# A SwiGLU FFN split into two stages: gate and up by Strassen's seven block products, down summed whole in PSUM

## The chip, the core and the metric

The kernel runs on one core of one Trainium2 chip. The metric is the time of one execution on the device in microseconds (us). Engines are named as in the profile: PE is TensorE's matmul, PEld its weight load, DVE is VectorE, ACT is ScalarE, POOL is GpSimd, SP is SyncE, whose queue issues nearly all DMAs.

## The reference, cut to what matters

One layer of a transformer-like trunk with 256 context tokens and 2048 latent tokens, D = 1024 features and D_FF = 2816 hidden features, all in float32. The token mixer is the same in both kernels; the change is in the last four lines.

```python
def rmsnorm(x, g):
    y = x * lax.rsqrt(jnp.mean(x * x, axis=-1, keepdims=True) + EPS)
    return y * g

def sandwich_block(x, mod, g_norm, mixer, w_gu, w_down):
    sh1, sc1, gt1, sh2, sc2, gt2 = mod
    h = rmsnorm(x, g_norm[0]) * (1.0 + sc1) + sh1
    m, extra = mixer(h)
    x = x + gt1 * rmsnorm(m, g_norm[1])
    h = rmsnorm(x, g_norm[2]) * (1.0 + sc2) + sh2
    gate, up = jnp.split(h @ w_gu, 2, axis=-1)       # (2304, 1024) @ (1024, 2 * 2816)
    f = (jax.nn.silu(gate) * up) @ w_down            # (2304, 2816) @ (2816, 1024)
    x = x + gt2 * rmsnorm(f, g_norm[3])
    return x, extra
```

## The kernel before

Every float32 operand of a large product is split into a high part (`F32R`, a copy by ACT) and a low part (the rest, a subtraction by DVE); `split` does both. A product is three matmuls for each 128 features of its contraction (`mm3`: high by high, high by low, low by high), summed in PSUM. All matmuls are recorded on one line, L37, since they go through the helper `InOrder`; the tile names tell them apart.

The program runs the input projection (`phase_b`, `phase_ac`), the three token mixers, the output projection (`phase_out`) and the FFN (`phase_ffn`) one after the other. `phase_out` writes the FFN's input, transposed (features on the partitions), to DRAM in six blocks of 384 tokens (`h2_d`), and the residual stream to `x1_d`. While it runs, `ffn_ahead` loads the first block and the first weights.

`phase_ffn` takes the 2304 tokens in three passes of 768 (`tb`), each of two blocks of 384 (`b`). The 22 chunks of 128 hidden features are taken in groups of four (the last has two). For each chunk `ffn_w` loads and splits 1024 x 128 weights of gate and as many of up (tiles `GH`, `GL`), and `product` makes, for each block, a gate tile and an up tile in PSUM (`p`, 24 matmuls each, 128 weights by 384 tokens), then `sg` = silu(gate) * up, and its two parts `ah`, `al` in SBUF. After a group, its four chunks are contracted with the rows of `w_down` (`dh`, `dl`): for each of 6 token tiles and 2 column halves twelve matmuls of 512 columns into `pd`, which DVE then adds to an accumulator in SBUF (`fa`, L1796 and L1798). After the last group `finish` norms, scales, adds the residual and stores the token tile.

The order: tiles come from pools that rotate over a fixed number of buffers, and the scheduler of the tile framework sets the order on each engine by priority and readiness, except where an `InOrder` engine is switched on (`pe.on`, `sp.on`), whose instructions keep the order of the program. Before, PE's is off in `phase_ffn`. Every engine takes its own queue strictly in order.

## Time and profile before

| | |
|---|---|
| time, median of 3 runs | 3910.35 us (3907.43 to 3915.01) |
| the profiled execution: span from first to last instruction | 3906.9 us; the page gives no separate time for it |
| TensorE clock granted, mean | 0.983 |
| PE busy | 3730.9 us, 95% |
| PEld busy | 3293.7 us, 84% |
| DVE, ACT, POOL busy | 2019.6, 1544.1, 376.4 us |
| the FFN in the span | about 2229 us to the end |

Busy time of PE is the sum of the durations of pipelined matmuls whose ends are modelled, so the distance between two starts is the better price of a matmul. In a group line, the first number after the bar is the busy time of all its instructions in us, the second the mean of one in ns. In the view by stretches, each engine's busy us is followed by its number of instructions.

### The profile page before, as it was taken

To read this page: it belongs to the slowest core of one execution; us is meant where nothing else is said; L and a number is where in the kernel's file an instruction comes from. 1 tells how busy PE (TensorE), PEld (TensorE's weight loads), DVE (VectorE), ACT (ScalarE), POOL (GpSimd) and SP (SyncE) were. 2 spreads that over 40 slices of the span, in tenths; PEclk is the share of its full clock that TensorE was granted. 3 is DMA by queue.
4 is the path that set the end of the run, shared out by engine and by line. 5 is a ranking of instruction groups with operands and counts; after the bars stand their busy time and mean duration, and the time that the engine had idled before them with its cause. 6 is when DMAs were issued, how large, how long until landed. Compare 5 with 4: busy or idle time off the path is not lost.

```text
span 3906.9 us, 64049 instructions
## 1 busy us (share of the span) xinstructions
PE 3730.9 (95%) x25318; PEld 3293.7 (84%) x25318; DVE 2019.6 (52%) x4488; ACT 1544.1 (40%) x3184; POOL 376.4 (10%) x691
## 2 busy tenths in 40 slices
PE   8997989879999999899999999999999999999998
PEld 5887889867777777688877899999999999999997
DVE  4794576689655555478755433333533323533323
ACT  4223322246666666557756522222322112322221
POOL 0002322620000000010024200000000000000000
PEclk9998999989999999999999999999999999999999
DMA  7556877741211111264336532222521122522211
GB/s 265 204 199 190 259 212 218 191 108 46 55 51 51 51 51 51 67 176 109 86 115 206 185 103 65 65 65 64 166 67 60 60 60 66 171 65 65 60 60 54
DMA packets 580862, 436.07 MB, mean 112 GB/s; under 512 B 247042, under 2 KB 519793, under 8 KB 578385
## 3 DMA queue, kind: packets, MB, share of 16 engines
q1 hardware_dynamic: 577776, 428.37, 36.7%
q8 instruction: 199, 3.26, 0.4%
q10 hardware_dynamic: 2624, 3.55, 0.3%
q14 instruction: 103, 0.84, 0.1%
q0 software_dynamic: 160, 0.05, 0.0%
HBM read 313.80 MB, written 118.05 MB: 111 GB/s over the span
## 4 chain that ended last, share of the span: by engine, by line
PE 48%; issue 31%; DVE 10%; ACT 4%; DMA 4%; POOL 3%; SPq 1%; POOLq 0%; ACTq 0%; DVEq 0%
PE p L37 9%; PE pso L37 8%; PE pt L37 7%; PE po L37 6%; PE pd L37 5%; PE rx L37 3%; DVE stmp L843 2%; PE Sa L37 2%; PE Sb L37 2%; PE S L37 2%; DVE mx L1220 2%; DVE sW L844 1%; PE m L37 1%; ACT P L1228 1%; DMA y<-oa 1%
## 5 line engine op out<-in xcount | busy, mean ns | idle before, releaser
L37 PE MATMUL p<-fhi,GH 128*128 128x384 f32 x2112 | 711.0, 337 | 5.1 <-DVE raw L1674 3.1
L37 PE MATMUL p<-flo,GH 128*128 128x384 f32 x2112 | 711.0, 337 | 0.3 <-DVE flo L1691 0.3
L37 PE MATMUL p<-fhi,GL 128*128 128x384 f32 x2112 | 710.0, 337 | 1.1 <-DVE GL L1691 1.1
L1034 ACT ACTIVATE PT<-pt 128x512 f32<-128x512 f32 (+1 forms) x600 | 332.3, 554 | 256.0 <-PE pt L37 249.2
L37 PEld LDWEIGHTS p<-fhi,GH 128*128 128x128 f32 x2112 | 397.3, 188 | 6.6 <-ACT raw L1623 3.3
L37 PEld LDWEIGHTS p<-fhi,GL 128*128 128x128 f32 x2112 | 397.3, 188 | 2.1 <-DVE GL L1691 1.8
L37 PEld LDWEIGHTS p<-flo,GH 128*128 128x128 f32 x2112 | 397.4, 188 | 1.7 <-DVE flo L1691 0.7
L1744 ACT ACTIVATE sg<-p 128x384 f32<-128x384 f32 x132 | 64.4, 488 | 681.0 <-PE p L37 681.0
L37 PE MATMUL po<-PT,V 128*64 128x256 f32 (+1 forms) x3072 | 314.8, 342 | 2.2 <-ACT PT L1034 1.9
L37 PE MATMUL pd<-dh,ah 128*128 128x512 f32 x792 | 309.3, 390 | 5.8 <-DVE fa L1798 5.5
L37 PE MATMUL pso<-whi,hi 128*128 128x384 f32 (+2 forms) x864 | 289.0, 334 | 26.2 <-ACT whi L255 13.7
L37 PE MATMUL pd<-dh,al 128*128 128x512 f32 x792 | 308.7, 390 | 0.0
L37 PE MATMUL pd<-dl,ah 128*128 128x512 f32 x792 | 308.5, 390 | 0.0
L1691 DVE TENSOR_TENSOR GL<-raw,GH 128x1024 fp32r<-128x1024 f32 x132 | 161.7, 1225 | 274.8 <-ACT GH L1690 274.6
L37 PE MATMUL pt<-ident,P 128*128 128x128 f32 x1752 | 284.9, 280 | 14.9 <-ACT PT L1034 7.9
L37 PE MATMUL pso<-whi,lo 128*128 128x384 f32 (+2 forms) x864 | 282.7, 327 | 6.4 <-DMA lo<-hl 6.3
L37 PE MATMUL pso<-wlo,hi 128*128 128x384 f32 (+2 forms) x864 | 282.7, 327 | 0.6 <-DVE wlo L256 0.5
L37 PEld LDWEIGHTS pt<-ident,P 128*128 128x128 f32 x1752 | 200.3, 141 | 94.3 <-ACT PT L1034 36.1
L1798 DVE TENSOR_TENSOR fa<-pd,fa 128x512 f32<-128x512 f32 x180 | 124.0, 690 | 264.9 <-PE pd L37 263.3
L37 PEld LDWEIGHTS po<-PT,V 128*64 128x64 f32 x3072 | 181.5, 137 | 79.3 <-issue 33.8
L1745 DVE TENSOR_TENSOR sg<-sg,p 128x384 f32<-128x384 f32 x132 | 73.0, 553 | 266.7 <-PE p L37 266.6
L1690 ACT ACTIVATE GH<-raw 128x1024 fp32r<-128x1024 f32 x132 | 139.8, 1061 | 144.8 <-PE p L37 125.6
(298 smaller groups left out, 6916.0 us busy)
## 6 DMA issues: line engine op xcount, KB each, us to landing
raw<-in_w_gu_dram SPq DMA_DIRECT2D x264, 256.0 KB, 3.6
raw<-in_w_down_dram SPq DMA_DIRECT2D x66, 512.0 KB, 3.7
wm<-in_w_mod_dram SPq DMA_DIRECT2D x48, 512.0 KB, 4.2
hi<-hh SPq DMA_DIRECT2D x36, 512.0 KB, 5.2
lo<-hl SPq DMA_DIRECT2D x36, 512.0 KB, 6.3
st<-ptk SPq DMA_DIRECT2D x18, 768.0 KB, 4.2
rst<-st SPq DMA_DIRECT2D x36, 384.0 KB, 5.3
hh<-hi SPq DMA_DIRECT2D x6, 1536.0 KB, 6.1
```

What stands on the lines that cost most here:

```text
L37: r = f(*x, **kw)
L843: v.tensor_tensor(tv, M[:n, c0:c1, c0:i], M[:n, c0:i, i].unsqueeze(1).to_broadcast([n, m, k]), ALU.mult)
L844: v.tensor_reduce(M[:n, c0:c1, i], tv, AX.X, ALU.add)
L1034: self.nc.scalar.activation(out, p, AF.Copy)
L1220: nc.vector.tensor_reduce(mx[:, i:i + 1], S[:, :hi_ - lo_], AX.X, ALU.max)
L1228: nc.scalar.activation(P[:, lo_:hi_], Ss[i][:, :hi_ - lo_], AF.Exp, bias=mx[:, 3:4], accum_out=sm[:, i:i + 1])
L1690: self.nc.scalar.activation(hi, raw, AF.Copy)
L1691: self.nc.vector.tensor_tensor(lo, raw, hi.bitcast(F32), ALU.subtract)
L1744: nc.scalar.activation(sg, ps[0], AF.Silu)
L1745: nc.vector.tensor_tensor(sg, sg, ps[1], ALU.mult)
L1798: nc.vector.tensor_tensor(facc[i][:, s], p, facc[i][:, s], ALU.add)
```

## The change

The FFN becomes two functions, `ffn_up` and `ffn_down`, with `silu(gate) * up` in DRAM between them (`a_d`, one tensor for each token tile).

`ffn_up` takes the same three passes of 768 tokens. For one chunk of 128 hidden features (one unit) the product is seen as a 2x2 block product: rows gate and up, contraction halves of 512 features, columns the two blocks of 384 tokens. Strassen's form in Winograd's variant needs seven block products of 12 matmuls (84 matmuls) in place of eight (96). Its operands are sums of blocks. Those of the weights are made for each unit: four POOL additions on 128x512 (`S`), and seven splits of 128x512 (`gop`, 10 buffers). Those of the tokens are made once for each pass by `prep_h` (`hop`, seven tiles without a second buffer, each filled in two halves `kk` of 128x768; temporaries `ht`, some of them made by POOL). The results are put together from three PSUM tiles X, Y and Z by five DVE additions of 384 columns that read PSUM (`p1`, `u2`, `u3`), two silus and a copy on ACT, and two POOL multiplications of 384 columns; six DMAs write the unit's result. PE keeps the order of the program: in it the last two products of a unit follow the first product of the next one, but not at the end of a pass.

`ffn_down` goes over the column halves `n` outermost. For each it loads and splits the 22 chunks of `w_down` once (`wd`, 24 buffers, raw tiles `wr` 4), and for every token tile `t` it loads and splits the activations in two pieces (`ar`, `ao`, 128x1408, 3 buffers) and sums 66 matmuls of 512 columns in one PSUM tile. The first half's result goes to DRAM (`f_d`); the second half's turn does the norm, the residual and the store. The program text of the other functions differs only by comments.

```diff
     def ffn_ahead(self, t):
         if 4 <= t < 12 and t % 2 == 0:
...
-        if t == 13:
-            self.first = [self.ffn_w(0, k4) for k4 in range(2)]
+        if t == 10:
+            self.sp.dma_start(self.hr1, self.h2_d[1])
+        if t == 12:
+            self.w_raw(0, self.wr0)
...
+    def ffn_up(self):
...
+            gp = es.enter_context(tc.tile_pool(name="u_g", bufs=10))
...
+            def prep_h(tb):
+                for kk in range(2):
...
+                    def put(n, x):
+                        self.split(H[n][:, 0, ks], H[n][:, 1, ks], x)
...
+                    t2 = tmp()
+                    tt(t2, B22, t1, ALU.subtract)
+                    put(6, t2)
+                    put(5, t1)
+                    t3 = tmp()
+                    gp_.tensor_tensor(t3, B22, B12, ALU.subtract)
+                    B21 = piece(0, 1)
+                    if tb:
+                        put(2, B21)
+                    put(7, t3)
+                    t4 = tmp()
+                    gp_.tensor_tensor(t4, B21, t2, ALU.subtract)
+                    put(4, t4)
+                    put(3, B22)
+            def prep_w(tb, f):
...
+                gp_.tensor_tensor(S[0], A21, A22, ALU.add)
+                gp_.tensor_tensor(S[1], S[0], A11, ALU.subtract)
+                gp_.tensor_tensor(S[2], A11, A21, ALU.subtract)
+                gp_.tensor_tensor(S[3], A12, S[1], ALU.subtract)
+                for n, x in ((1, A11), (6, S[1]), (5, S[0]), (2, A12), (7, S[2]), (4, A22), (3, S[3])):
+                    put(n, x)
+                return ops
+            def mm(p, w, h, first, last):
+                for k in range(4):
+                    for i, (s, m) in enumerate(((0, 0), (0, 1), (1, 0))):
+                        self.pe.matmul(p, lhsT=w[:, s, k], rhs=h[:, m, k], start=first and k == 0 and i == 0,
+                                       stop=last and k == 3 and i == 2, skip_group_check=True)
+            def units(tb, f):
...
+                mm(X, w[1], h[1], True, True)
+                yield
+                p1 = t("p1")
+                nc.scalar.activation(p1, X, AF.Copy)
...
+                mm(Y, w[6], h[6], True, True)
+                u2 = t("u2")
+                tt(u2, Y, p1, ALU.add)
+                mm(Z, w[5], h[5], True, True)
+                if tb or f:
+                    mm(X, w[2], h[2], False, True)
+                mm(Y, w[7], h[7], False, True)
+                u3 = t("u3")
+                tt(u3, Y, p1, ALU.add)
+                tt(u3, Z, u3, ALU.add)
+                yield
+                mm(Y, w[4], h[4], False, True)
+                mm(Z, w[3], h[3], False, True)
+                sg = t("sg")
+                nc.scalar.activation(sg, X, AF.Silu)
+                o = wk.tile([128, 2, BT], F32, tag="o", name="o")
+                tt(p1, Y, p1, ALU.add)
+                nc.gpsimd.tensor_tensor(o[:, 0], sg, p1, ALU.mult)
+                tt(u2, Z, u2, ALU.add)
+                nc.scalar.activation(u2, u2, AF.Silu)
+                nc.gpsimd.tensor_tensor(o[:, 1], u2, u3, ALU.mult)
+                for i in range(6):
+                    self.sp.dma_start(self.a_d[6 * tb + i][:, f, :], o[:, i // 3, 128 * (i % 3):128 * (i % 3) + 128])
+                yield
+            prev = None
+            for tb in range(3):
+                if prev:
+                    next(prev)
+                    prev = None
+                prep_h(tb)
+                for f in range(NF):
+                    u = units(tb, f)
+                    next(u)
+                    if prev:
+                        next(prev)
+                    next(u)
+                    prev = u
+            next(prev)
+    def ffn_down(self):
...
+            for n in range(2):
+                W = {}
+                for t in range(NT):
+                    p = ps.tile([128, 512], F32, tag="pd", name="pd")
+                    for j in range(2):
+                        x = a_load(t, j)
+                        for c in range(11):
+                            k = 11 * j + c
+                            if t == 0:
+                                W[k] = w_load(n, k)
+                            for i, (u, m) in enumerate(((0, 0), (0, 1), (1, 0))):
+                                self.pe.matmul(p, lhsT=x[:, u, c], rhs=W[k][:, m], start=(k == 0 and i == 0),
+                                               stop=(k == NF - 1 and i == 2))
...
     def run(self):
...
-            self.pe.on = False
-            self.phase_ffn()
+            self.pe.on = True
+            self.ffn_up()
+        self.ffn_down()
```

How the change moves the instructions, at the places that the prediction speaks of. First DVE's queue in the middle of a pass. Before, one chunk of hidden features (`sg` and `al` for each of two blocks, `GL` the low parts of the weights):

```order
L1691 TENSOR_TENSOR GL_24175<-raw,GH_24173 128x1024
L1745 TENSOR_TENSOR sg<-sg,p_29027 128x384
L1691 TENSOR_TENSOR GL_24176<-raw,GH_24174 128x1024
L1748 TENSOR_TENSOR al<-sg,ah 128x384
L1745 TENSOR_TENSOR sg<-sg,p_29092 128x384
L1748 TENSOR_TENSOR al<-sg,ah 128x384
```

Now one unit (`gop` are the low parts of the seven weight operands of the unit after the next, from `wr0` as loaded or from the sums `S`; the rows that read Y or Z put the results together):

```order
L1820 TENSOR_TENSOR u3_35559<-Y_35455,p1_35507 128x384
L1696 TENSOR_TENSOR gop_35713<-wr0_24174,gop_35713 128x512
L1821 TENSOR_TENSOR u3_35559<-Z_35456,u3_35559 128x384
L1696 TENSOR_TENSOR gop_35716<-S_35706,gop_35716 128x512
L1828 TENSOR_TENSOR p1_35507<-Y_35455,p1_35507 128x384
L1696 TENSOR_TENSOR gop_35719<-S_35705,gop_35719 128x512
L1830 TENSOR_TENSOR u2_35521<-Z_35456,u2_35521 128x384
L1696 TENSOR_TENSOR gop_35722<-wr0_24174,gop_35722 128x512
L1814 TENSOR_TENSOR u2_35661<-Y_35595,p1_35647 128x384
L1696 TENSOR_TENSOR gop_35725<-S_35707,gop_35725 128x512
L1696 TENSOR_TENSOR gop_35728<-wr0_24174,gop_35728 128x512
L1696 TENSOR_TENSOR gop_35731<-S_35708,gop_35731 128x512
```

Six instructions a chunk have become twelve a unit, and those that PE waits for stand between the splits. POOL, whose only work in the FFN before was two instructions on one column for each token tile, now has six large ones a unit:

```order
L1787 TENSOR_TENSOR S_28462<-S_28461,wr1_26637 128x512
L1832 TENSOR_TENSOR o_28251<-u2_28137,u3_28175 128x384
L1788 TENSOR_TENSOR S_28463<-wr1_26637 128x512
L1789 TENSOR_TENSOR S_28464<-wr1_26637,S_28462 128x512
L1786 TENSOR_TENSOR S_28601<-wr0_24174 128x512
L1829 TENSOR_TENSOR o_28391<-sg_28389,p1_28263 128x384
```

The sums of the weights and the products of the results stand in one queue. Second, DVE at the end of the first pass (`hop5`, `hop6` and `hop7` are the token operands 5, 6 and 7 of the next pass, and the tile named `hop1` is operand 2; `u2_29677` and `u3_29715` belong to the last unit of this pass):

```order
L1696 TENSOR_TENSOR hop6_26635<-ht_29763,hop6_26635 128x768
L1814 TENSOR_TENSOR u2_29677<-Y_29611,p1_29663 128x384
L1756 TENSOR_TENSOR ht_29782<-hr1_24173 128x768
L1696 TENSOR_TENSOR hop5_26634<-ht_29756,hop5_26634 128x768
L1696 TENSOR_TENSOR gop_29831<-S_29813,gop_29831 128x512
L1758 TENSOR_TENSOR ht_29789<-hr1_24173,ht_29782 128x768
L1696 TENSOR_TENSOR hop1_24172<-hr4_26638,hop1_24172 128x768
L1696 TENSOR_TENSOR hop5_26634<-ht_29782,hop5_26634 128x768
L1696 TENSOR_TENSOR hop7_26636<-ht_29769,hop7_26636 128x768
L1820 TENSOR_TENSOR u3_29715<-Y_29611,p1_29663 128x384
```

Seven instructions of the next pass stand between two additions that PE needs. Third, SP's queue where the first stage hands over to the second (`a_26611` to `a_26616` are the six token tiles of the last pass, `a_26599` the first token tile of all):

```order
L37 DMA a_26613<-o 128x128
L37 DMA wr<-in_w_down_dram 128x512 x2
L37 DMA a_26614<-o 128x128
L37 DMA a_26615<-o 128x128
L37 DMA a_26616<-o 128x128
L37 DMA wr<-in_w_down_dram 128x512 x3
L37 DMA ar<-a_26599 128x1408
L37 DMA wr<-in_w_down_dram 128x512 x4
```

Before, at the first group of the FFN, SP had the weights of both products and the residual's tiles behind each other, and no write that a load waits for:

```order
L1787 DMA fgt<-gate_d 128x1024
L37 DMA raw<-in_w_gu_dram 128x4x128 x6
L1753 DMA x<-x_2_18662 128x1024
L37 DMA raw<-in_w_gu_dram 128x4x128 x2
L1781 DMA raw<-in_w_down_dram 128x1024 x4
```

The first load of activations now stands behind the last writes of the stage before.

More of the change, by code (lines that the diff above doesn't have):

```diff
@@ L1676, in ffn_early @@
     def ffn_early(self, pool):
-        self.ffn_h = [[pool.tile([128, KD, BT], F32R, name=f"f{n}0") for n in ("hi", "lo")]]
-        self.GH = [pool.tile([128, 4, 2, 128], F32R, name=f"GH{i}") for i in range(2)]
-        self.GL = [pool.tile([128, 4, 2, 128], F32R, name=f"GL{i}") for i in range(2)]
-        self.gu = 0
+        self.hop0 = [pool.tile([128, 2, 4, BT], F32R, name=f"hop{i}") for i in range(2)]
+        self.hr1 = pool.tile([128, KD, BT], F32, name="hr1")
+        self.wr0 = pool.tile([128, 4, 512], F32, name="wr0")
     def ffn_ahead(self, t):
         if 4 <= t < 12 and t % 2 == 0:
-            self.ffn_h_load(0, 0, t - 4)
-        if t == 13:
-            self.first = [self.ffn_w(0, k4) for k4 in range(2)]
+            k = t - 4
+            raw = self.raw()[:, :2 * BT].rearrange("p (k t) -> p k t", k=2)
+            self.sp.dma_start(raw, self.h2_d[0][:, k:k + 2])
+            op = self.hop0[k // 4]
+            self.split(op[:, 0, k % 4:k % 4 + 2], op[:, 1, k % 4:k % 4 + 2], raw)
+        if t == 10:
+            self.sp.dma_start(self.hr1, self.h2_d[1])
+        if t == 12:
+            self.w_raw(0, self.wr0)
     def split(self, hi, lo, raw):
@@ new lines, in ffn_down, with a_load @@
+            cst = es.enter_context(tc.tile_pool(name="d_c", bufs=1))
+            wp = es.enter_context(tc.tile_pool(name="d_w", bufs=2))
+            wk = es.enter_context(tc.tile_pool(name="d_k", bufs=2))
+            ps = es.enter_context(tc.tile_pool(name="d_p", bufs=4, space=PSUM))
+            gt = cst.tile([128, 2, 1024], F32, name="fgt")
+            ss = cst.tile([128, 2, NT], F32, name="fss")
+            A = {}
+            W = {}
+            def a_load(t, j):
+                raw = wk.tile([128, 11, 128], F32, tag="ar", name="ar", bufs=3)
+                self.sp.dma_start(raw, self.a_d[t][:, 11 * j:11 * j + 11])
+                op = wk.tile([128, 2, 11, 128], F32R, tag="ao", name="ao", bufs=3)
+                self.split(op[:, 0], op[:, 1], raw)
+                return op
@@ new lines, in w_load @@
+            def w_load(n, c):
+                raw = wp.tile([128, 512], F32, tag="wr", name="wr", bufs=4)
+                self.sp.dma_start(raw, a["w_down"][0, 128 * c:128 * c + 128, 512 * n:512 * n + 512])
+                w = wp.tile([128, 2, 512], F32R, tag="wd", name="wd", bufs=NF + 2)
+                self.split(w[:, 0], w[:, 1], raw)
+                return w
+            for n in range(2):
+                s = slice(512 * n, 512 * n + 512)
+                W = {}
+                for t in range(NT):
[9 more added lines that the diff above has]
+                                               stop=(k == NF - 1 and i == 2))
+                    if n == 0 and t == 0:
@@ L1786, in phase_ffn @@
                         for r in range(2):
                             nc.sync.dma_start(gt[:, r, :], self.gate_d[1, r:r + 1, :].to_broadcast([128, 1024]))
-                    for i in range(6):
-                        c = slice(128 * i, 128 * i + 128)
-                        for n in range(2):
-                            s = slice(512 * n, 512 * n + 512)
-                            p = psd.tile([128, 512], F32, tag="pd", name="pd")
-                            self.mm3(p, [x[:, c] for x in AH], [x[:, c] for x in AL], [x[:, s] for x in DH],
-                                     [x[:, s] for x in DL])
-                            if gi == 0:
-                                nc.vector.tensor_copy(facc[i][:, s], p)
-                            else:
-                                nc.vector.tensor_tensor(facc[i][:, s], p, facc[i][:, s], ALU.add)
-                        if last:
-                            finish(6 * tb + i, facc[i])
+                    junk = wk.tile([128, 512], BF16, tag="junk", name="junk", bufs=1)
@@ new lines, in ffn_down @@
+                    nc.scalar.activation(junk, p, AF.Square, accum_out=ss[:, n, t:t + 1])
+                    if n == 0:
+                        f = wk.tile([128, 512], F32, tag="f", name="f")
+                        nc.vector.tensor_copy(f, p)
+                        nc.sync.dma_start(self.f_d[t], f)
+                        continue
+                    v = 0 if t < NLAT else 1
+                    x = wk.tile([128, 1024], F32, tag="x", name="x")
+                    f = wk.tile([128, 512], F32, tag="f", name="f")
@@ new lines, in ffn_down @@
+                    self.sp.dma_start(x, self.x1_d[t])
+                    self.sp.dma_start(f, self.f_d[t])
+                    s1 = wk.tile([128, 1], F32, tag="s1", name="s1")
+                    nc.gpsimd.tensor_tensor(s1, ss[:, 0, t:t + 1], ss[:, 1, t:t + 1], ALU.add)
+                    r = self.rstd(wk, s1, 1, 1.0 / D, "rs")
+                    g = wk.tile([128, 512], F32, tag="g", name="g")
+                    nc.vector.scalar_tensor_tensor(f, f, r, gt[:, v, 0:512], ALU.mult, ALU.mult)
```

139 lines of the change are left out of this document (61 added, 78 removed).

## The prediction

> **What bounds the kernel now.** I read the page's first part, then the chain of waits, then the table by stretches over the FFN.
>
> ```profile
> span 3906.9 us, 64049 instructions
> PE 3730.9 (95%) x25318; PEld 3293.7 (84%) x25318; DVE 2019.6 (52%) x4488; ACT 1544.1 (40%) x3184; POOL 376.4 (10%) x691
> ...
> 2335.99 67.12 PE p L37 x384
> 2403.10 32.69 PE pd L37 x144
> ...
> 2000.00:2235.00 235.00, 228.38 (x1136) 190.54 (x1135) 114.22 (x139) 138.56 (x342) 83.43 (x147) 0.99 0.54 178
> ...
> 2235.00:3893.60 1658.60, 1649.40 (x8696) 1550.41 (x8694) 575.60 (x724) 366.88 (x518) 13.43 (x32) 1.00 0.26 78
> ```
>
> The chain shows one group of four chunks: 384 matmuls for gate and up, 174.8 ns from start to start, then 144 of the down product, 227.0 ns each. The last row holds the FFN: of 1658.6 us PE is busy 1649.4, DVE 576, POOL 13, at a full clock, with 78 GB/s moved. The row above it is the output projection, in which `ffn_ahead` runs: PE is busy there 228 of 235 us. So the FFN lasts as long as its matmuls: three passes of 5.5 groups, 16.5 x 99.81 = 1646.9 us. The edges:
>
> ```profile
> 2224.56 1.91 PE L37 MATMUL pst<-ident,xn 128*128 128x128 f32 x16
> 2229.59 0.66 PE L37 MATMUL p<-fhi,GH 128*128 128x384 f32 x1 [3.12 <-DVE raw L1674]
> 2232.29 0.44 PE L37 MATMUL p<-fhi,GL 128*128 128x384 f32 x1
> 2232.57 0.33 PE L37 MATMUL p<-fhi,GH 128*128 128x384 f32 x1
> 2234.09 2.91 ACT L1623 ACTIVATE raw<-pst,b,s 128x128 f32<-128x128 f32 x8 [0.93 <-PE pst L37]
> 3893.29 0.40 PE L37 MATMUL pd<-dh,al 128*128 128x512 f32 x1
> 3895.42 0.19 ACT L1671 ACTIVATION_READ_ACCUMULATOR rjunk<-fa 128x1 f32 x1
> ...
> 3899.79 0.19 POOL L89 TENSOR_SCALAR rsm<-rss 128x1 f32<-128x1 f32 x1 [3.27 <-ACT rjunk L1671]
> 3900.06 0.55 POOL L91 TENSOR_TENSOR rsr<-rsm,mhalf 128x1 f32<-128x1 f32 x1
> 3901.97 1.23 DVE L1674 TENSOR_TENSOR x<-x,fa 128x1024 f32<-128x1024 f32 x1
> ```
>
> I count from 2224.6, where the output projection's products end, to the end of the span: 1682.3 us, of which 1646.9 are matmuls and 35.4 everything else (the start, small waits, and 13.2 after the last matmul).
>
> **The matmuls.** Removed: a unit has 84 instead of 96, so 66 x 84 x 0.1748 = 969.1 us stand for 66 x 96 x 0.1748 = 1107.5: 138.4 us less. The down product keeps 2376 matmuls of 512 columns, 539.4 us. The 216 DVE copies and additions of `fa` go (0.69 us each, beside matmuls of the next group; what PE waited for them is within the 35.4). What PE gains is paid back wherever the other engines make it wait. Their prices:
>
> ```profile
> L1691 DVE TENSOR_TENSOR GL<-raw,GH 128x1024 fp32r<-128x1024 f32 x132 | 161.7, 1225 | 274.8 <-ACT GH L1690 274.6
> L1745 DVE TENSOR_TENSOR sg<-sg,p 128x384 f32<-128x384 f32 x132 | 73.0, 553 | 266.7 <-PE p L37 266.6
> L1691 DVE TENSOR_TENSOR flo<-raw,fhi x24: 942/958/959, 2071.7 to 3324.4; 128x768 fp32r<-128x768 f32 x24
> L1690 ACT ACTIVATE GH<-raw 128x1024 fp32r<-128x1024 f32 x132 | 139.8, 1061 | 144.8 <-PE p L37 125.6
> L1744 ACT ACTIVATE sg<-p 128x384 f32<-128x384 f32 x132 | 64.4, 488 | 681.0 <-PE p L37 681.0
> L790 POOL TENSOR_TENSOR prd<-prd,mi x18: 1262/1292/1831, 399.5 to 605.9; 128x512 f32<-128x512 f32 x18
> L1553 POOL TENSOR_TENSOR y<-o,bg x18: 724/735/746, 1904.1 to 2199.7; 128x256 f32<-128x256 f32 x18
> 399.55 1.29 POOL L790 TENSOR_TENSOR prd<-prd,mi 128x512 f32<-128x512 f32 x1
> 399.62 1.77 DVE L740 TENSOR_TENSOR py<-py,prr 128x512 f32<-128x512 f32 x1 [2.45 <-POOL prr L738]
> 403.79 0.69 DVE L744 TENSOR_TENSOR pkt<-py,begc 128x512 f32<-128x512 f32 x1 [1.08 <-PE ptr L37]
> 1023.85 1.59 POOL L971 TENSOR_TENSOR rSe<-rS,eh 64x128 f32<-64x128 f32 x4 [23.66 <-DVE rS L1003]
> 1023.36 0.87 DVE L1003 TENSOR_TENSOR rS<-rSe,rx 64x256 f32<-64x256 f32 x2 [0.34 <-PE rx L37]
> ```
>
> In the rows with a slash the numbers are least, median and longest ns. A DVE subtraction of 128x512 from SBUF costs 0.69 us (L744), of 128x768 0.96, an addition of 384 columns from PSUM 0.55. On POOL 512 columns cost 1.29, and on the line through 256 columns (0.735) 384 cost 1.01 and 768 cost 1.85. Splits on ACT lie between the silu's 0.49 at 384 and 1.06 at 1024: 0.60 at 512. And the two engines get in each other's way: L740, begun 0.07 us after POOL's L790, took 1.77 instead of 0.69 and ended 0.55 after POOL did. L1003, with one input in PSUM, did not suffer.
>
> **A unit in the middle of a pass.** PE needs 84 x 0.1748 = 14.68 us. DVE: 7 x 0.69 + 5 x 0.55 = 7.6. ACT: 7 x 0.60 + 3 x 0.49 = 5.7. POOL: 4 x 1.29 + 2 x 1.01 = 7.2. Laid out from the end of the product Y7, with each engine's queue in its order and every split waiting for a POOL instruction that is under way, `u3` ends at 0.75 and PE wants it at 2.1, when the next unit's first product ends; the second `u3` ends at about 2.5 of 4.2; POOL's run of sums starts at 8.0, when the third split is done, and the last split ends at 14.75, just before the next Y7. The splits are for the unit after the next, so only the `u` rows are urgent. I take no stall: 0. Reserve is 1.3 us, so a stall stays possible; at 0.3 us a unit it would be 20. SP issues nine DMAs a unit, three weight loads and six writes, at 0.34 to 0.50 us (rows below) about 4 us of 14.7; the writes stand ahead of the weights of the unit after, and a weight load that lands as in the rows below has 2 us in hand. They carry 1.4 MB, 95 GB/s; the page's first slice moved 265. In the output projection the weights' four splits of 1024 columns go and 2.6 MB of loads come earlier, both beside its matmuls: 0, from -2 to 3.
>
> **The start.** Before, the first weights were split ahead; now ACT's first split waits until the last L1623 ends (2237.0), and its DVE half ends 1.3 later. Until the second half of Y6's token operand is ready, DVE has 9 splits of 512 and 11 instructions of 768 columns in its queue: 6.2 + 10.6 = 16.8 us, so 2254.4. If POOL's sums of that time (ten of 512 columns, three or four of 768, some 18 us) come in between one by one, 2272. PE has done two and a half products (5.2 us) by then. The dead time from 2224.6 is thus 24.6 to 42.6; since L740's row says that these instructions don't overlap, I take 37.
>
> **The two seams between passes.** Per seam DVE has 14 splits of `hop` and two differences, 16 x 0.96 = 15.3 us, and POOL 3.7, on top of a unit's 7.6 and 7.2. The tiles have no second buffer, so this can't be done early; the `u3` of the pass's last unit stands behind seven of these rows, and at the seam no product of a next unit covers it. DVE alone takes 22.9 - 14.7 = 8.2 more than a unit's time of PE; with POOL in series 19.1. Splits of the units to come have some reserve. Taken: 14 each, 28; 5 to 20 each.
>
> **The handover.**
>
> ```profile
> raw<-in_w_gu_dram SPq DMA_DIRECT2D x264, 256.0 KB, 3.6
> raw<-in_w_down_dram SPq DMA_DIRECT2D x66, 512.0 KB, 3.7
> st<-ptk SPq DMA_DIRECT2D x18, 768.0 KB, 4.2
> L1781 SPq DMA_DIRECT2D raw<-in_w_down_dram x62: 327/340/366, 2355.0 to 3808.4; - x62
> L37 SPq DMA_DIRECT2D raw<-in_w_gu_dram x238: 367/499/1568, 2303.4 to 3792.0; - x119
> ...
> GB/s 265 204 199 190 259 212 218 191 108 46 55 51 51 51 51 51 67 176 109 86 115 206 185 103 65 65 65 64 166 67 60 60 60 66 171 65 65 60 60 54
> ```
>
> After the last matmul of `ffn_up`: addition, silu and POOL product 2.1, three writes to issue 1.0, their landing about 3 (below the 3.6 of a 256 KB transfer), since the first `ar` waits for it; its 704 KB take 4.1; its split 1.4 on ACT and 1.7 on DVE. That is 13 us without a matmul. Then the 22 chunks of `w_down` come through four raw tiles: 3.6 to land, 0.60 and 0.69 to split, 1.2 us a chunk, where PE wants one each 3 x 0.227 = 0.68; nine are there in time, the rest costs about 4. Taken: 17. Between 12 (the wait for the writes falls away) and 32 (the chunks come at 1.2 from the start). After that a token tile is 66 x 0.227 = 15.0 us of PE, with at most 5.4 of DVE (two splits of 1408 columns at 1.65, three steps of 0.69) and 3.5 of ACT beside it: 0. The second column half loads its 22 chunks during the last token tile of the first, two slots ahead: 2, from 0 to 6.
>
> **Clock and end.** After 3.1 us without a matmul, nine of them came 0.32 us apart (2229.59 to 2232.29), 1.3 us lost; after the start and the handover that happens again: 3 in all. The Trainium skill ("TensorE: Matmul & The Clock Gate", part 1) gives half rate for the first 3.4 us after an idle window of 3.4 us; by that the two gaps would cost an estimated 3.4 us, and by this row 2.6. At the end only 512 columns are left: square 0.6 and 0.2, three small POOL steps 1.1, two DVE steps 1.4, the store as before (3903.2 to 3906.9, 3.7), some 0.5 between them: 7.5 instead of 13.2.
>
> **The sum.** 37 + 0 + 28 + 17 + 2 + 3 + 7.5 = 94.5 stands against 35.4: 59.1 more. 138.4 - 59.1 = 79.3 us gained: a span of 3827.6. The median of the runs lies 3.4 above the profiled span, so 3831 us.
>
> **Rivals.**
> 1. *DVE and POOL in series set the pace.* 7.6 + 7.2 = 14.8 us a unit, already PE's 14.68; DVE's queue also waits for ends of products. For it speaks L740's row, and that the splits and POOL's sums make up 12.0 of the 14.8. Against it: the five additions read PSUM, as L1003 does, and can run beside POOL. It eats the gain when a unit grows by 79.3/66 = 1.2 us, to 15.9. With waits of 1.8 on top it gives 3831 + 119 = 3950: slower. The Trainium skill ("SBUF — State Buffer", section "Who interferes with whom") states it as a rule: a VectorE instruction with two SBUF inputs and a GpSimd one that reads SBUF exclude each other for the whole instruction. Taken as far as it goes the rule speaks for this rival; the trace agrees at 1.77 against 0.69.
> 2. *The engines meet rarely.* The start costs 25, the seams 6 each, the handover 13: 12 + 16 + 4 = 32 us less, 3799. Against it: at start and seams both queues are full.
> 3. *The handover is bound by its loads.* All chunks at 1.2 us and both column halves alike: 32 + 12 instead of 19, 3856. For it: weights and activations come through one queue. Against it: the first slices of the page move 265 GB/s, a chunk each 1.2 us is 218.
> 4. *The product saves nothing*, because X, Y and Z, rewritten in turns, hold PE up at each of seven products by 0.3 us: 139 us, 3970. Nothing in the profile speaks for it; DVE's addition from PSUM ends in time above.
>
> **Chances.** Forecast 0.52, rival 1 0.10 (0.07 beyond its break-even), rival 2 0.18, rival 3 0.14, rival 4 0.02, rival 1 just at its break-even 0.04. The forecast's own range is 3810 to 3855. The range of 8 in 10 takes in rival 2's time with a little more (3790) and rival 3's with 0.4 us of stall a unit (3885). Two tenths of a per cent, 8 us, is about what a measurement of this kernel can tell from no change. Faster 0.52 + 0.03 + 0.18 + 0.14 = 0.87, the same 0.04, slower 0.07 + 0.02 = 0.09.
>
> **What would show it.** In the profile of after: 5544 matmuls of 384 columns at 174.8 ns in the chain within a unit, and units 14.7 apart (else rival 1: PE waits for `u3` in each unit, DVE's `gop` rows well above 0.69 on average). Means of `gop` near 1.2 would show that the engines exclude each other; near 0.7 rival 2. A gap on PE of some 10 us at Y6 of the first unit, one at each seam on `u3` or operand 2, one of 13 before the first `pd` of the new stage. The prediction is wrong most easily if POOL's instructions cost more beside DVE than alone, since the reserve in a unit is 1.3 us.

## The result, and the profile after

The changed kernel takes 3839.73 us (median of 4 runs, 3837.47 to 3842.02) where the kernel before takes 3908.89 beside it (3901.4 to 3915.01): ratio 0.9823, 95% interval 0.9810 to 0.9837. It is faster by 69 us; predicted were 3831 with a range of 3790 to 3885. The head of the page after, with busy time, share of the span and number of instructions of each engine:

```profile
span 3835.5 us, 64839 instructions
PE 3607.6 (94%) x24526; PEld 3166.5 (83%) x24526; DVE 2308.8 (60%) x4786; ACT 1723.1 (45%) x3552; POOL 966.3 (25%) x1135
```

The FFN again is PE's to bound. In the table by stretches, two stretches inside a pass (after each engine's busy us its instructions, then the granted clock, the DMA share and GB/s):

```profile
2445.00:2545.00 100.00, 100.00 (x576) 100.00 (x575) 61.30 (x83) 38.92 (x69) 54.52 (x41) 1.00 0.35 98
2955.00:3225.00 270.00, 270.00 (x1551) 270.00 (x1551) 164.85 (x222) 105.11 (x186) 146.05 (x110) 1.00 0.32 93
```

PE has no idle moment there; the first product of a unit stands 14.64 us after that of the unit before (predicted 14.7). What time there is without a matmul lies at the edges. PE's timeline, only the rows that wait, at the start, at the two seams, at the handover and at the second column half:

```profile
2217.18 1.91 PE L37 MATMUL pst<-ident,xn 128*128 128x128 f32 x16
...
2229.77 1.01 PE L37 MATMUL X<-hop,gop 128*128 128x384 f32 x2 [2.66 <-ACT gop L1695]
2234.89 3.57 PE L37 MATMUL X<-hop,gop 128*128 128x384 f32 x10 [4.11 <-DVE gop L1696]
2241.50 3.69 PE L37 MATMUL X<-hop,gop 128*128 128x384 f32 x12 [3.04 <-ACT p L1809]
...
2256.02 0.69 PE L37 MATMUL Y<-hop,gop 128*128 128x384 f32 x1 [9.78 <-ACT hop L1695]
2260.71 1.97 PE L37 MATMUL Y<-hop,gop 128*128 128x384 f32 x5 [4.00 <-DVE hop L1696]
...
2579.43 3.69 PE L37 MATMUL Y<-hop,gop 128*128 128x384 f32 x12 [3.99 <-DVE u L1820]
2597.34 1.97 PE L37 MATMUL X<-hop,gop 128*128 128x384 f32 x5 [4.61 <-DVE hop L1696]
2914.56 4.21 PE L37 MATMUL Y<-hop,gop 128*128 128x384 f32 x12 [3.99 <-DVE u L1820]
2933.42 1.57 PE L37 MATMUL X<-hop,gop 128*128 128x384 f32 x5 [4.30 <-DVE hop L1696]
...
3246.31 2.37 PE L37 MATMUL Y<-hop,gop 128*128 128x384 f32 x12 [0.65 <-DVE u L1820]
3265.80 1.22 PE L37 MATMUL pd<-wd,ao 128*128 128x512 f32 x2 [15.03 <-DMA wr<-in_w_down_dram]
3267.46 10.75 PE L37 MATMUL pd<-wd,ao 128*128 128x512 f32 x37 [0.44 <-DVE ao L1696]
3279.54 0.51 PE L37 MATMUL pd<-wd,ao 128*128 128x512 f32 x1 [1.33 <-ACT wd L1695]
...
3294.65 65.61 PE L37 MATMUL pd<-wd,ao 128*128 128x512 f32 x281 [0.23 <-DVE wd L1696]
3565.21 4.83 PE L37 MATMUL pd<-wd,ao 128*128 128x512 f32 x12 [2.99 <-ACT wd L1695]
```

How these rows are turned into dead time, against the prediction's terms:

| term | predicted | measured | from |
|---|---|---|---|
| start | 37 | 38.1 | 2260.71 - 2217.18, less 31 matmuls (5.4) |
| stall in units | 0 | 0 | PE 100% busy in the stretches |
| two seams, and the last unit | 28 | 26.9 | second seam's Y less first seam's: 335.13, less 22 units of 14.64, is 13.05; a like first one; 0.8 at the end of the last pass |
| handover | 17 | 29.5 | 15.2 to the first `pd`, then 28.85 to 3294.65 for 64 matmuls (14.5) |
| second column half | 2 | 6.2 | the wait shown, two shorter ones, slow matmuls |
| clock | 3 | 2.0 | 17 matmuls from 2260.71 take 4.98 us instead of 3.0; the other slow ones are in the terms above |
| end | 7.5 | 8.4 | last `pd` at 3827.1 |
| sum | 94.5 | 111.1 | |

The FFN's 1618.3 us (see below) less 66 units of 14.64 and the down product's 539.4 leave 112.7, so 1.6 us are in no row.

So the FFN, counted as in the prediction from the end of the output projection's products (the first row above) to the end of the span, fell from 1682.3 to 1618.3 us, 64 of the predicted 79; the other 7 us of the span are in front of it. I call this count the FFN's length below. Stretches ahead of it vary by some microseconds between profiles of the same code, so the length compares variants better than spans do. It isn't exact either: from the end of the last gate/up product to the end of the span, after and the five kernels below with the same `ffn_down` (plain, sums_dve, all_dve, pool_twice, seam) took 577.8 to 584.9 us in one profile each, and after is the longest of them.

### The profile page after: what moved, and what is told of

It is laid out like the page before. It is cut to its first block, busy times and chain, and to the rows that moved or that the text cites. A ratio compares the mean times of both kernels' runs of the same rounds, so it can differ in the third digit from the quotient of the medians.

```text
span 3835.5 us, 64839 instructions
## 1 busy us (share of the span) xinstructions
PE 3607.6 (94%) x24526; PEld 3166.5 (83%) x24526; DVE 2308.8 (60%) x4786; ACT 1723.1 (45%) x3552; POOL 966.3 (25%) x1135
## 5 line engine op out<-in xcount | busy, mean ns | idle before, releaser
L37 PE MATMUL pd<-wd,ao 128*128 128x512 f32 x2376 | 550.3, 394 | 26.1 <-DMA wr<-in_w_down_dram 15.0
L37 PEld LDWEIGHTS pd<-wd,ao 128*128 128x128 f32 x2376 | 450.6, 190 | 125.7 <-ACT ao L1695 15.4
L37 PE MATMUL Y<-hop,gop 128*128 128x384 f32 x2376 | 452.3, 338 | 22.4 <-ACT hop L1695 9.8
L37 PEld LDWEIGHTS Y<-hop,gop 128*128 128x128 f32 x2376 | 422.1, 191 | 24.2 <-ACT hop L1695 10.1
L1696 DVE TENSOR_TENSOR gop<-S,gop 128x512 fp32r<-128x512 f32 x264 | 235.6, 893 | 167.3 <-ACT gop L1695 157.6
L37 PE MATMUL X<-hop,gop 128*128 128x384 f32 x1584 | 306.2, 342 | 18.7 <-DVE hop L1696 8.9
L37 PEld LDWEIGHTS X<-hop,gop 128*128 128x128 f32 x1584 | 283.5, 190 | 20.8 <-DVE hop L1696 9.6
L37 PE MATMUL Z<-hop,gop 128*128 128x384 f32 x1584 | 297.7, 336 | 0.0
L37 PEld LDWEIGHTS Z<-hop,gop 128*128 128x128 f32 x1584 | 278.7, 189 | 0.1
L1696 DVE TENSOR_TENSOR gop<-wr,gop 128x512 fp32r<-128x512 f32 x198 | 200.9, 1015 | 83.8 <-ACT gop L1695 77.6
```

The costliest lines, as they stand in the source:

```text
L37: r = f(*x, **kw)
L1696: self.nc.vector.tensor_tensor(lo, raw, hi.bitcast(F32), ALU.subtract)
```

## The experiments

Eleven kernels were run, each beside the kernel before on the same chip. "After" is the changed kernel; the FFN's length is from the profile. The medians of the kernel before lie between 3904.64 and 3908.89 on these chips, so kernels are to be compared by the ratio.

| kernel | median us | ratio to before, 95% interval | FFN's length |
|---|---|---|---|
| after | 3839.73 | 0.9823, 0.9810 to 0.9837 | 1618.3 |
| plain | 3934.45 | 1.0073, 1.0058 to 1.0088 | 1709.3 |
| sums_dve | 3810.96 | 0.9759, 0.9742 to 0.9775 | 1589.4 |
| all_dve | 3805.58 | 0.9737, 0.9722 to 0.9751 | 1582.8 |
| pool_twice | 3916.26 | 1.0019, 1.0010 to 1.0029 | 1692.8 |
| seam | 3833.43 | 0.9812, 0.9797 to 0.9827 | 1609.5 |
| raw8 | 3825.57 | 0.9792, 0.9777 to 0.9807 | 1603.3 |
| early | 3824.43 | 0.9784, 0.9769 to 0.9798 | 1601.7 |
| combo | 3799.18 | 0.9717, 0.9703 to 0.9732 | 1574.0 |
| combo_early | 3793.58 | 0.9704, 0.9688 to 0.9721 | 1570.8 |
| best | 3786.99 | 0.9691, 0.9677 to 0.9706 | 1566.1 |
| best_warm | 3788.73 | 0.9698, 0.9683 to 0.9712 | 1565.5 |

### What the seven products are worth: plain

```diff
-    gp_.tensor_tensor(S[0], A21, A22, ALU.add)    # and three more sums, seven splits
+    for i in (1, 2, 0, 3):                        # the four weight blocks, split as they are
...
+    for b, (lo, hi) in enumerate(((1, 2), (4, 3))):
+        mm(X, w[0], H[lo], True, False)           # gate
+        mm(X, w[1], H[hi], False, True)
+        mm(Y, w[2], H[lo], True, False)           # up
+        mm(Y, w[3], H[hi], False, True)
```

> The two-stage form without Strassen: each unit makes its gate and up tiles directly, eight block products (96 matmuls of 384 columns), four weight splits and no POOL sums; the token operands need four splits of two halves per pass instead of seven and three sums. Theory of the prediction: the middle of a pass is PE alone, so the seven products are worth 66 x 12 x 0.1748 = 138 us there, and their price is what the start and the two seams cost beyond this form. Start here: only two or four splits stand between the last norm and the first products, dead time about 15 instead of 38; seams 2 x 8 instead of 2 x 13. So 3840 + 138 - 23 - 10 = 3945, i.e. about 35 us slower than the kernel before, because the hand-over, the loads of the second half and the end stay as in the changed kernel. Rival (the product gains little inside a unit, the time comes from the two-stage form, which drops the accumulation of the down product in SBUF): about 3840 to 3870 here.

Measured: 0.73% slower than before, 91 us more FFN than after. Its timeline at the start, and then at the handover:

```profile
2240.43 1.01 PE L37 MATMUL X<-hop,gop 128*128 128x384 f32 x2 [9.36 <-DMA wr<-in_w_gu_dram]
2241.91 5.47 PE L37 MATMUL X<-hop,gop 128*128 128x384 f32 x22 [0.47 <-DVE gop L1696]
...
3360.75 4.87 PE L37 MATMUL pd<-wd,ao 128*128 128x512 f32 x12 [10.55 <-ACT wd L1695]
```

The first `Y` follows at 2247.22; from the end of the output projection's products (2221.14) that is 21.9 us of dead time for 24 matmuls, and it is the load of the weights that PE waits for, not DVE. At the seams PE waits for nothing at all. The four splits cost 0.69 us each here, POOL being idle. The expectation had 15 us at the start and 8 at each seam, where there are 21.9 and none. So the two-stage form by itself makes the FFN 27 us longer than before (1709.3 against 1682.3), and the seven products are worth 91 on top: 141 of the matmuls (a unit takes 16.77 us here, 14.64 in after), less 45 by which the start and the seams are longer in after (67.2 against 22.1 us of the gate/up stage beyond its units), less 4.5 by which everything behind the last gate/up product was shorter in plain. The prediction's balance holds in kind, and the rival that the product saves nothing is out.

### Where the edges come from: sums_dve, all_dve, pool_twice

The first moves POOL's sums to DVE, the second POOL's two products as well, the third makes POOL's weight sums twice:

```diff
-    gp_.tensor_tensor(S[0], A21, A22, ALU.add)             # sums_dve: all four S, t3 and t4
+    tt(S[0], A21, A22, ALU.add)
...
-    nc.gpsimd.tensor_tensor(o[:, 0], sg, p1, ALU.mult)     # all_dve: and both products
+    tt(o[:, 0], sg, p1, ALU.mult)
...
     gp_.tensor_tensor(S[0], A21, A22, ALU.add)             # pool_twice: on the changed kernel
+    gp_.tensor_tensor(S[0], A21, A22, ALU.add)             # each of the four once more
```

> All sums of weight blocks (four a unit) and of token blocks (two a half) go from POOL to DVE; POOL keeps only the two products of 384 columns a unit. Exclusion theory (DVE and POOL instructions with SBUF inputs run one after the other): the mean of the weight splits on DVE falls from 0.89 and 1.02 us to 0.70 to 0.75, since POOL's 1.29 us instructions no longer stand in their way, and a sum costs 0.69 instead of 1.29, so start and seams get shorter or stay: start 38 to about 30, seams 13 to about 10 each, 3825 to 3835. Rival (POOL works beside DVE most of the time): the means stay near 0.9, DVE's queue is longer by ten sums of 0.69 and four of 0.96 at the start and by four of 0.96 and more at each seam: start 38 to about 48, seams 13 to 17, 3855 to 3860. In the middle of a pass both expect PE without a gap (DVE 7.6 + 2.8 = 10.4 of 14.68 us a unit).

> All sums and also the two products silu(gate) * up of a unit go to DVE, so that POOL does nothing in the gate/up stage. DVE then has 7.6 + 4 x 0.69 + 2 x 0.55 = 11.5 us of work in a unit of 14.68. With the sums alone on DVE (3811) the second sum still took 1.28 us on average instead of 0.69, beside POOL's product. Exclusion theory: that sum falls to 0.69, every row of splits to 0.69 and 0.96, seams get a little shorter (7.5 to about 6): 3805 to 3811. Rival (DVE's queue gets too long, additions that PE waits for come late): PE waits for u in each unit, 0.3 us or more: 3830 and above.

> The changed kernel with each of POOL's four sums of weight blocks in a unit made twice, one right after the other (the second writes the same tile again), nothing else. POOL then has 8 x 1.29 + 2 x 1.01 = 12.3 us of work in a unit of 14.68, less than PE's. Exclusion theory: POOL's 12.3 and DVE's seven splits of 0.69 (and none of the five additions that read PSUM) can't run at the same time, 12.3 + 4.8 = 17.2 us a unit, so PE waits about 2.5 us in each unit: 66 x 2.5 = 165 us more, about 4005, slower than the kernel before. This is the first rival of the prediction, brought about on purpose. Rival (the engines only slow each other a little, each is bound by its own work): POOL fits in, units stay at 14.7, start and seams lengthen by some 10 us each: 3840 to 3870.

The groups of DVE's splits (busy us, mean ns, idle before), first of after, then of sums_dve, then of all_dve:

```profile
L1696 DVE TENSOR_TENSOR gop<-S,gop 128x512 fp32r<-128x512 f32 x264 | 235.6, 893 | 167.3 <-ACT gop L1695 157.6
L1696 DVE TENSOR_TENSOR gop<-wr,gop 128x512 fp32r<-128x512 f32 x198 | 200.9, 1015 | 83.8 <-ACT gop L1695 77.6
```

```profile
L1696 DVE TENSOR_TENSOR gop<-S,gop 128x512 fp32r<-128x512 f32 x264 | 184.6, 701 | 162.3 <-ACT gop L1695 156.6
L1696 DVE TENSOR_TENSOR gop<-wr,gop 128x512 fp32r<-128x512 f32 x198 | 135.8, 686 | 45.1 <-ACT gop L1695 45.0
L1787 DVE TENSOR_TENSOR S<-S,wr 128x512 f32<-128x512 f32 x66 | 84.5, 1281 | 2.0
```

```profile
L1787 DVE TENSOR_TENSOR S<-S,wr 128x512 f32<-128x512 f32 x66 | 45.3, 686 | 0.0
```

With POOL's sums gone the splits fall to 0.69 and 0.70 us, and the one sum that still meets POOL's product takes 1.28 until that goes too: then 0.69. The same instruction on the same data thus costs between 0.69 and 1.28 by what POOL does. Giving DVE four sums more a unit made the FFN 28.9 us shorter, where the exclusion theory expected 5 to 15 and its rival 15 to 20 in the other direction; all_dve came out where the theory had it. Of the 28.9, 7.6 lie at the start (to the end of the fifth product), 14.2 at the seams (7.5 between the two, instead of 13) and 7.1 behind the last gate/up product. The last are not explained by the edit, which changes nothing in that stage, and may be no more than the scatter of single profiles given above. So 21.8 are what the edit is shown to do; by the ratios the gain is 0.64%, 25 us. With the products on DVE too a seam is down to 2.3 us: 2569.25 to 2893.63 is 324.4 for 22 units.

pool_twice is the prediction's first rival made on purpose, and it turns the gain into a loss of 0.19%: POOL has 12.3 us of work in a unit by durations alone, less than PE, and yet it is full (busy 149.6 of the 160 us from 2400 to 2560) and PE waits. A stretch of DVE, then of POOL, and PE's rows that wait for `u3` in two units:

```profile
2457.49 1.31 DVE L1696 TENSOR_TENSOR gop<-S,gop 128x512 fp32r<-128x512 f32 x1
...
2459.20 1.32 DVE L1696 TENSOR_TENSOR gop<-wr,gop 128x512 fp32r<-128x512 f32 x1
```

```profile
2456.51 1.74 POOL L1790 TENSOR_TENSOR S<-wr 128x512 f32<-128x512 f32 x1
2458.34 1.63 POOL L1791 TENSOR_TENSOR S<-wr 128x512 f32<-128x512 f32 x1
2459.92 1.73 POOL L1792 TENSOR_TENSOR S<-wr,S 128x512 f32<-128x512 f32 x1
2461.73 1.63 POOL L1793 TENSOR_TENSOR S<-wr,S 128x512 f32<-128x512 f32 x1
2463.95 1.30 POOL L1786 TENSOR_TENSOR S<-wr 128x512 f32<-128x512 f32 x1 [0.59 <-DVE gop L1696]
```

```profile
2466.32 2.36 PE L37 MATMUL Y<-hop,gop 128*128 128x384 f32 x12 [0.79 <-DVE u L1824]
2481.70 2.36 PE L37 MATMUL Y<-hop,gop 128*128 128x384 f32 x12 [0.46 <-DVE u L1824]
```

Four sums, each with one split between, take 2456.51 to 2463.36, 1.71 us a pair, against 1.29 + 0.69 = 1.98 one after the other. So both theories' numbers were off: the engines do take turns, but about 0.27 us of a pair overlaps, and a unit comes to 15.4 us there (the two rows of `Y`, which wait for `u3`), where full exclusion gave 17.2. Of the 74 us by which the FFN grew, some 50 are 0.75 in each of 66 units; the rest is at the start and the seams, where waits of 12 us appear. The Trainium skill ("SBUF — State Buffer", section "Who interferes with whom") has the blocked engine stand still for the whole instruction of the other; these rows agree with the turns, and put the blocked time of a pair at some 0.27 us below the sum of the two durations.

### The seam: seam

```diff
-    if prev:
-        next(prev)
-        prev = None
-    prep_h(tb)
+    hs = prep_h(tb)               # with one raw token tile more
+    next(hs)                      # operand 1 alone for a later pass
     for f in range(NF):
         u = units(tb, f)
         next(u)                   # first product of the new unit
         if prev:
             next(prev)            # last two of the unit before
+        if tb and f == 0:
+            next(hs)              # the other operands
```

> At the two seams the last unit's final two products stand behind the next pass's first product on PE, as inside a pass; only the split of the first token operand is recorded ahead of them. Theory A (the first gap of a seam, 4.0 us and 1.5 to 2.1 us more of half-rate matmuls behind it, comes from the missing cover of u3): with 2.1 us of cover the gap is 2 us and too short to lose the clock, 13 falls to about 9 per seam: 3831. Theory B (the work of DVE and POOL for the new operands sets the seam's length, wherever PE waits): the second gap grows by what the first one loses, 13 stays: 3839.

Measured: the FFN 8.8 us shorter, of which 2.6 are behind the last gate/up product, where the edit changes nothing; by the count between the seams (2579.03 to 2910.62) 9.5 us each instead of 13. By the ratios alone (0.9812 against 0.9823) it can't be told from no change. Its waits at the first seam:

```profile
2579.03 2.36 PE L37 MATMUL Y<-hop,gop 128*128 128x384 f32 x12 [1.36 <-DVE u L1828]
2593.55 3.92 PE L37 MATMUL Y<-hop,gop 128*128 128x384 f32 x12 [3.81 <-DVE u L1822]
2601.58 2.32 PE L37 MATMUL Y<-hop,gop 128*128 128x384 f32 x12 [2.01 <-DVE u L1828]
```

The gap on `u3` falls from 3.99 to 1.36, and the product behind it takes 2.36 instead of 3.69: it keeps the clock. But a wait of 3.81 and one of 2.01 come up later, both on DVE. Theory A gives the size (9), and B's wait does appear, in part: DVE is late either way, which sums_dve cures better.

### The handover: raw8 and early

```diff
-    raw = wp.tile([128, 512], F32, tag="wr", name="wr", bufs=4)
+    raw = wp.tile([128, 512], F32, tag="wr", name="wr", bufs=8)         # raw8
...
+    if tb == 2 and f == 20:                                             # early (bufs=7)
+        self.sp.dma_start(self.ar_e, self.a_d[0][:, :11])
+        for c, raw in enumerate(self.wr_e):                             # three chunks
+            self.sp.dma_start(raw, self.a["w_down"][0, 128 * c:128 * c + 128, 0:512])
```

> Eight raw tiles for the chunks of w_down instead of four. Theory A (the loads are a loop of four tiles: issue, 4.6 us to land, 1.3 to split, so four chunks per 6 us, 1.5 us each, where PE wants one per 0.68): with eight tiles 0.75 us a chunk, the waits for splits after the first down product fall from 14.3 to about 4 us and those at the second column half from 6.2 to about 1: 3825. Theory B (the DMA engines are the limit at the hand-over: 12.2 MB in 46 us, 265 GB/s, busy in eight to nine tenths of the time): more loads in flight only land later; at most 2 us less at the hand-over, and 4 us at the second half, where only some 130 GB/s move: 3834 to 3840.

> Eight raw tiles become seven, but the first activations (token tile 0, written two passes earlier) and the first three chunks of w_down are loaded during the last pass, into the space of the raw token tiles, which stays reserved. Theory A (the 12 to 15 us without a matmul at the hand-over are a chain: the tiles of the new stage come free, loads are issued, land, are split): only the splits remain, 0.6 and 0.7 for a chunk, 1.4 and 1.6 for the activations: the gap falls from 12.7 (eight tiles) to about 4, 3825.6 - 8 = 3817. Theory B (what counts is when the 19 other chunks arrive, since PE consumes a chunk in 0.68 us and they come in 0.75 or more): the wait only moves behind the first three chunks: 3823 to 3826.

raw8 made the FFN 15 us shorter, and what lies behind the last gate/up product 9 to 16 us shorter than in the six kernels with the `ffn_down` of after: theory A's place, and about its size. In after SP issues a chunk when a raw tile comes free, four at a time; in raw8 six and eleven stand together. SP's timeline of after, then of raw8, and raw8's PE:

```profile
3258.24 5.95 SPq L37 DMA_DIRECT2D wr<-in_w_down_dram  x4
3264.24 0.43 SPq L37 DMA_DIRECT2D ar<-a  x1
3268.03 2.55 SPq L37 DMA_DIRECT2D wr<-in_w_down_dram  x4
...
3274.25 2.34 SPq L37 DMA_DIRECT2D wr<-in_w_down_dram  x4
```

```profile
3260.34 3.42 SPq L37 DMA_DIRECT2D wr<-in_w_down_dram  x6
3263.81 0.64 SPq L37 DMA_DIRECT2D ar<-a  x1
3265.06 10.97 SPq L37 DMA_DIRECT2D wr<-in_w_down_dram  x11
```

```profile
3266.57 1.22 PE L37 MATMUL pd<-wd,ao 128*128 128x512 f32 x2 [12.40 <-DMA wr<-in_w_down_dram]
3268.23 16.89 PE L37 MATMUL pd<-wd,ao 128*128 128x512 f32 x64 [0.44 <-DVE ao L1696]
3287.84 0.73 PE L37 MATMUL pd<-wd,ao 128*128 128x512 f32 x2 [2.72 <-ACT ao L1695]
```

Four chunks in some 6 us is the 1.5 us a chunk of theory A. With eight tiles no matmul of the first token tile waits for a chunk once the first has come; the dead time of the handover falls from 29.5 to 20.2, counted in the same way, and the second half's wait is gone. The DMA engines then move 377 GB/s at full use just after the first issues (3262 to 3267), where after moved 235 to 297 in three stretches from 3258 to 3295. So the four tiles were the limit, and the engines are the next one.

early agrees: the first `pd` comes 7.1 us after the last product instead of 12.4, but a wait of 1.95 for a chunk and one of 3.06 for the next token tile's activations follow, and the handover as a whole is 18.9 instead of 20.2. That is theory B: the first chunks were not what bounded it.

### Together: combo, combo_early, best, best_warm

combo is sums_dve, raw8 and seam; combo_early adds the early loads; best adds the products on DVE and puts the gate rows, 1 MB of loads, behind more of the activations'; best_warm fills the handover's gap with matmuls on a constant:

```diff
-    if n == 0 and t == 0:        # best: the gate rows, 2 x 512 KB
+    if n == 0 and t == 4:
...
+    for i in range(48):          # best_warm, between the stages
+        self.pe.matmul(X, lhsT=self.ident, rhs=self.ident, start=True, stop=True)
```

> Three edits together: sums on DVE, eight raw tiles, the cover of the seam. If their gains are in different places they add up: 28.8 + 14.2 + 6.3 less than the changed kernel's 3839.7 is 3790. Rival (the seam's two edits share the same gap: with the sums on DVE the first gap is already 2.3 instead of 4.0 us; the hand-over's wait had already fallen by 2 us): 3797.

> The three edits (sums on DVE, raw tiles, cover of the seam) and the early loads of the hand-over. By theory A of the early loads 8 us less than the three edits give, about 3783; by theory B about the same as the three edits, 3788 to 3790.

> The three edits and the early loads, and also the two products of a unit on DVE and the loads of the gate rows (1 MB) moved from the first to the fifth token tile of the down stage. The products take 0.55 us on DVE instead of 1.01 on POOL and no longer stretch the second sum; the seams had 1.9 us left, the hand-over 18. Expected 2 to 5 us less than without the two last edits (3793.6): 3789 to 3792. Rival (nothing more to get there, since PE no longer waits for DVE): 3794.

> As the kernel with all edits, with 48 matmuls of 128 columns on a constant between the two stages, about 6 us of the 7 us in which PE waits for the first chunk of w_down; their result is not used. Theory (a gap of 7 us costs full clock: the granted clock was 0.50 in the first 4 us of the down stage and 0.68 in the next, and 59 matmuls took 16.65 us instead of 13.4): the first matmuls of the down stage come 0.227 us apart at once; 3 us less, or less than that where the chunks then come too late. Rival (the slow matmuls there wait for operands, not for the clock): no change.

combo shortened the FFN by 44.3 us where its three edits alone sum to 52.7, and its 3799 us lie next to the rival's 3797. But at the seams nothing is shared. Up to the end of the last gate/up product the edits save 27.2 us one by one (sums_dve 21.8, seam 6.2, raw8 -0.8) and 29.5 together; 1.9 us a seam remain. What is missing lies behind that product: 25.6 one by one (7.1, 2.6 and 15.9), 14.8 together. There after's profile is the longest of its kind, and each of the three savings is counted from it. By the ratios the edits alone save 1.06% of the kernel before, and combo saves the same 1.06% against after. So the gains add up within the noise, and the rival's shared gap is not borne out. Plain addition meets its number too, once each median is set against the kernel before that ran beside it (3908.89, 3904.64 and 3907.61), which the expectation's 3790 did not do. The early loads took 3 more, nearer to theory B. best is 3787 us, 3.1% below the kernel before and 1.3% below the changed one by the ratios; the handover came down from 18.4 to 14.4, most of it because the second token tile's activations no longer stand behind the gate rows (its first product waited 3.53 us for them in combo_early, 0.98 here). best_warm gave nothing. The stretches of PE around its handover, and what stands in the gap:

```profile
3225.00:3229.00 4.00, 4.00 (x39) 1.00 0.79 244
3229.00:3233.00 4.00, 4.00 (x38) 1.00 1.00 276
```

```profile
3223.18 10.88 PE L37 MATMUL X<-ident 128*128 128x128 f32 x96
3234.16 15.20 PE L37 MATMUL pd<-wd,ao 128*128 128x512 f32 x64
```

The clock stayed at 1.00 up to 3249, where in best it was 0.50 from 3229 to 3237, and 64 matmuls took 15.20 us where best has 61 in 15.92. But the filling took 10.9 us, not 6 (each of its matmuls is two on the engine), so the first `pd` came later, and both kernels reach the continuous part 29.8 us after the last product. The premise on the clock was right; the gain wasn't there to have, because the end of the handover is set by loads: the second token tile's product waits 1.05 us for a split of activations on ACT, which itself waits for their load. A filling of the right length wasn't tried.

## Why the prediction was right, and which term was mis-sized

- **The matmuls**: 138.4 us forecast; units are 14.64 apart for 14.68, 16.78 before (67.12 for four), which makes 141, and no stall. The reserve of 1.3 us at `u3` held in after, and pool_twice shows how near it was: 5 us of POOL time more a unit use it up.
- **Start and seams**: 38.1 for 37 and 26.9 for 28. The gap at Y6 of the first unit (9.78) and at each seam those on `u3` (3.99) and on operand 2 (4.61 and 4.30) stand where it put them, and the reason given, DVE and POOL in turns, is borne out by sums_dve and all_dve. As a test on its own the prediction's choice between means of `gop` near 1.2 and near 0.7 was too coarse: 0.89 and 1.02 are a mixture, since in a unit POOL works about half the time.
- **The handover is the step that failed**: 17 predicted, 29.5 measured. Its first part, 13 us without a matmul, was 15.2. Its second, "nine are there in time, the rest costs about 4", was 14.3: a chunk came every 1.5 us, not every 1.2, because four raw tiles are a loop of landing (4.6 here, 3.6 was taken) and splitting, and because no chunk was begun before the gate/up stage had ended: its last product ends at 3250.6, the first load is issued at 3251.9, and ACT had split five chunks, not nine, when the first `pd` came. That the gate/up stage has to give its space free first is seen in ACT's timeline of combo_early, where the chunk had been loaded long before and its split still waited for the last product (to 3224.9). In after that load also stands in SP's queue behind writes of the last unit, so which of the two held it there is open:

```profile
3225.11 1.15 ACT L1694 ACTIVATE wd<-hr 128x512 fp32r<-128x512 f32 x2 [6.67 <-PE Z L37]
```

  In four other kernels with the same `ffn_down` (sums_dve, all_dve, pool_twice, seam) the same count gives 25.9 to 27.6, so the miss is 9 to 12.5 us. This comes near the third rival's handover of 32, not its 12 for the second half, and by another mechanism: it blamed the loads' rate, and raw8 shows it was the number of tiles first. The prediction's working was loose here by its own prices too: 13 late chunks at 1.2 us against 0.68 cost up to 6.8 and not 4, and all chunks at 1.2 from the start come to 13 + 22 x 0.52 = 24.4 and not 32. About 2.4 of the 14.3 are slow matmuls (37 took 10.75 us instead of 8.4; the granted clock was 0.50 until 3270), for which the sum had its own term.
- **The second column half**, 6.2 for 2, is the same loop; eight tiles take it away.
- **The end**, 8.4 for 7.5. Its last rows:

```profile
3829.93 1.26 POOL L1916 TENSOR_TENSOR x<-x,f 128x512 f32<-128x512 f32 x1 [0.86 <-DVE f L1914]
3830.55 1.20 DVE L1917 TENSOR_TENSOR x<-x,g 128x512 f32<-128x512 f32 x1
```

  Half of the miss is L1917, 1.20 instead of 0.69 beside POOL's L1916: the effect that the prediction used at the start and forgot at the end.
- **The output projection**, costed at 0 (-2 to 3), ended 7.4 us earlier in the profile. 2.6 are within it, where the first weights' splits are gone; the rest is ahead of any changed code. The end of its products lies between 2216.2 and 2223.1 in the twelve profiles with the new stages, 2219.5 in the mean, so a single profile is uncertain here by 3 us, and the span's miss of 7.9 us (3835.5 for 3827.6) is two errors that partly cancel: some 15 too little for the edges, some 7 too much in front. That the total came so close is luck in this part.
- **Rival 2**, that the engines meet rarely, is out with the start and the seams as long as forecast; **rival 1** is what pool_twice made of the kernel.

## What to carry to other kernels

When a fast-multiplication scheme trades matmuls for additions, count the saving in the steady state and then walk the edges, since the additions that hide in the middle are bare at every start and seam. Before sums are given to an idle POOL, look whether DVE runs two-input instructions from SBUF beside it: here four extra sums on the busier DVE made the kernel 0.6% faster. A stage that begins with loads needs enough raw tiles for its first chunks to be in flight together; a rate of chunks that equals tiles over latency shows up as blocks of issues as large as the pool.

## What was not expected of the hardware

- DVE and POOL with inputs in SBUF take turns, but a pair of instructions of 0.69 and 1.29 us costs 1.71, not 1.98.
- Two gaps of the same length, 2.31 us, in one kernel (sums_dve) had different ends; the products behind them at the two seams:

```profile
2570.95 2.35 PE L37 MATMUL Y<-hop,gop 128*128 128x384 f32 x12 [2.31 <-DVE u L1820]
...
2900.51 3.92 PE L37 MATMUL Y<-hop,gop 128*128 128x384 f32 x12 [2.31 <-DVE u L1820]
```

  The first ran at full rate, with the granted clock at 1.00 all through; the second lost 1.6 us, with the clock at 0.50 from 2902 to 2904. The gaps of 3.99 us at the seams of after, raw8 and early cost 1.4 to 2.9 each over the two products behind them. The Trainium skill ("TensorE: Matmul & The Clock Gate", part 1) puts the loss of the clock after an idle window of about 3.4 us that runs freely; this case agrees that it does not depend on the gap's length alone, since two gaps of 2.31 us ended differently, but one of them shows half rate after a gap shorter than that window, and the measurement decides. The expectation of seam, that a gap of 2 us is too short to lose the clock, was not safe by this.
